# Five units of two down-projections computed with seven block products instead of eight

## The chip, the cores and the metric

The kernel runs on one core of a Trainium2 chip. The metric is the device time of one execution in microseconds, as the median of three runs. Engines are named as the profile names them: PE (TensorE, matrix products), DVE (VectorE), ACT (ScalarE), POOL (GpSimd) and SP (which only issues transfers here). A weight load on TensorE has a row of its own, PEld.

## What is computed

The reference is a small decoder trunk in float32 on 256 tokens of 1024 features: a layer with block-sparse attention, then a layer with sliding-window attention that reads shared keys and values, and behind each attention a channel mixer. The change touches only the last product of the channel mixer:

```python
def conv_ffn(h, w_up, conv_w, conv_b, w_down):
    S_ = h.shape[1]
    u = h @ w_up                                   # 1024 -> 2 x 2816
    up = jnp.pad(u, ((0, 0), (CONV_W - 1, 0), (0, 0)))
    u = conv_b + sum(conv_w[j] * up[:, j:j + S_] for j in range(CONV_W))
    gate, val = jnp.split(u, 2, axis=-1)
    return (jax.nn.silu(gate) * val) @ w_down      # 2816 -> 1024

for l in range(DEPTH):
    ...
    x = x + o.transpose(0, 2, 1, 3).reshape(B_, S_, N_HEADS * HEAD_DIM) @ w_o
    x = x + conv_ffn(rmsnorm(x, ffn_norm[l]), w_up[l], conv_w[l], conv_b[l], w_down[l])
return rmsnorm(x, final_norm)
```

## The kernel before

**Numbers in two parts.** TensorE multiplies in a 32-bit format of reduced precision (fp32r). Every operand is therefore split: a high part, the value rounded to fp32r, and a low part, the rest. A product takes three matmuls: high x high, high x low, low x high. ScalarE makes high parts (`hi_part`, L181, for weights), VectorE low parts (`lo_part`, L189; L191 where a gain is multiplied in).

**Weights in units.** All weights are packed on the host into units of 128 x 2048 floats. SP fetches a unit into one of three raw buffers (`fetch`, L166 to L170). `prepare` (L197) queues its splitting in two or four cuts. The high and low parts lie in four buffers each (`weights`, L193), so a unit's parts can be made once the unit four before it is used up: `used(i)` (L219) calls `prepare(i + 4)`, and `need(i)` sees to it that a unit's steps are queued before TensorE reads it. `w_time` (L203) spaces the due times of units by 4500 ns of the model's clock or more.

**Order.** The program is written by one pass that keeps a model's clock: `tick` advances it by the length of the matmuls issued, `chain` queues steps of the other engines with a delay each, and a step is written down when the clock passes its due time; `require` forces a chain that is needed now. From attention on, the framework's scheduler may take ready instructions of an engine earlier than they were written. Each engine runs its own list in order.

**A mixer** (`ffn`, L661). 22 up units: each gives 128 gate and 128 value features for all 256 tokens, in 48 matmuls of 256 columns (L680 to L682) into a bank of PSUM (tags `u`, `t`, at first `acc`). `post` (L700) takes the convolution and the gate: ScalarE L715, VectorE L719 and L721, ScalarE's silu L725, the product on GpSimd L726, then its high part on ScalarE (L730) and its low part on VectorE (L731), into a quad: a buffer of 128 x 1024 floats in the pool `qd`, which has 15 of them. A quad `pq` holds the parts of two up units. The scaled input of the mixer lies in four more quads until the last up unit has read it.

**A down-projection** (`Down`, L569). 11 units; unit i holds two blocks of 128 rows (k = 0, 1) of `w_down`, 1024 columns each, in two halves (n = 0, 1). The 256 tokens are two blocks (b = 0, 1). So a unit is eight products of 128 x 128 by 128 x 512: A(b,k) B(k,n), summed over k and over all units into four banks `acc[b][n]`. `mm` (L576) writes three matmuls of 512 columns for each (L587, L588, L590); `units` runs through units 0 to 8 and `finish` (L601) takes units 9 and 10 in an order that completes one bank after the other. `add` (L652, instruction L656) adds a bank to the residual `xr[b]`, and `after` starts the next norm: squares (L321), transposes (L288), the split (L297, L298). Behind the first mixer follows the projection of keys and values (L345 to L347) with two weight units of its own; behind the second the final norm: POOL multiplies by the gain (L1057), rstd (L330), ScalarE writes one half of the output (L1068), and `tail` (L1071) the last quarter.

**Names.** `U_DN0` and `U_DN1` number the first units of the two down-projections, `U_KV` the units behind the first. `bank(tag)` hands out PSUM banks: two `u`, two `t`, four `acc`. `mid()` hands out 128 x 512 buffers.

Of the kernel before, what the change touches and what calls it, by code (L numbers as in the profile page):

```python
# [14 lines left out]
P = 128  # L15
# [37 lines left out]
U_KV = U_DN0 + NF // 2  # L53
# [4 lines left out]
N_UNITS = U_DN1 + NF // 2  # L58
# [3 lines left out]
def trunk(ctx: ExitStack, tc, x, xw, pos, cpk, fin, w, out):  # L62
# [116 lines left out]
    def hi_part(i, c):  # L179
        g = gain_of(i, c)  # L180
        nc.scalar.activation(wq[i][0][:, c], raws[i][:, c], AF.Copy, **({} if g is None else {"scale": g}))  # L181

    def lo_part(i, c):
        g, raw, hi, lo = gain_of(i, c), raws[i][:, c], f(wq[i][0][:, c]), wq[i][1][:, c]
# [12 lines left out]
    def prepare(i):  # L197
# [371 lines left out]
    class Down:  # L569


        def __init__(self, u, n_u, parts, wait, short=False):
            self.u, self.n_u, self.parts, self.wait, self.short = u, n_u, parts, wait, short
            self.acc = None

        def mm(self, i, k, b, cols, last=1):  # L576
            if self.acc is None:
                self.acc = [[bank("acc") for _ in range(2)] for _ in range(NB)]
            need(self.u + i)
            self.wait(i)  # L580
            hi, lo = wq[self.u + i]
# [10 lines left out]

        def units(self, lo, hi):
            for i in range(lo, hi):
                for k in range(2):
# [3 lines left out]
                used(self.u + i)  # L599

        def finish(self, i0, after, tail=None, by_half=False):  # L601
# [26 lines left out]
            for i in range(i0, self.n_u):  # L628
                used(self.u + i)

        def end(self, b, n, tail):
# [5 lines left out]
            need(self.u + i)  # L637
            self.wait(i)
            wh, wl = wq[self.u + i]
# [21 lines left out]
    def ffn(layer, u_up, u_dn, hT, y, rb, after, tail=None):  # L661
# [38 lines left out]
        def post(i, up, pq):  # L700
            hi, lo = pq[:, 2 * (i % 2)], pq[:, 2 * (i % 2) + 1]
            t = [row3(S) for _ in range(2)]
            gs, h = row3(S), row3(S)
# [24 lines left out]
            steps = [(200.0, scale), (700.0, tap2)] if i < n_raw else [(200.0, tap2)]  # L728
            chain(("p", i), *steps, (400.0, taps), (1600.0, gate),
                  (3400.0, lambda: nc.scalar.activation(hi, h, AF.Copy)),  # L730
                  (450.0, lambda: nc.vector.tensor_tensor(out=lo, in0=h, in1=f(hi), op=ALU.subtract)))  # L731
            parts.append((hi, lo))

# [10 lines left out]
        for i in range(2, NF):  # L744
            if i % 2 == 0:
                pq = quad()
# [5 lines left out]
        def wait(i):  # L752
            require("p", 2 * i)
            require("p", 2 * i + 1)

        if tail is not None:
            nc.sync.dma_start(fin_t, fin.partition_broadcast(P))
        dn = Down(u_dn, NF // 2, parts, wait, tail is not None)
# [347 lines left out]
def pack(inp):  # L1106
# [20 lines left out]
    def rows2(mat):  # L1127
        mm = k_major(mat)
        for i in range(mm.shape[0] // 2):
            units.append(turns(mm[2 * i:2 * i + 2]).transpose(1, 0, 2).reshape(P, UNIT))  # L1130
# [61 lines left out]
```

## Time and profile before

| | us |
|---|---|
| three runs, median (lowest to highest) | 547.5 (547.49 to 548.63) |
| profiled execution, span from first to last instruction | 545.6 |
| PE busy in that span | 537.5 |
| VectorE / ScalarE / GpSimd busy | 416.9 / 372.6 / 131.6 |
| granted TensorE clock, mean | 0.998 |

The profiled execution is one of its own; what is known of its time is its span, 1.9 us under the median of the runs. Rows of the profile give line, engine, operation, the written and read buffers by the program's names, the shape, and count; then busy time in total, the mean of one in ns, and the idle time before with what ended it. Rows of the order of time begin with the start and the length in us, and end with the idle time before, in brackets. A matmul's length is its latency: matmuls overlap, so what one costs is the distance between starts.

### The profile page before, as it was taken

The page shows a single profiled execution, that of the slowest core. Times are in us where ns is not written, and L with a number is a line of the kernel's source. Part 1 is how long each engine was busy: PE and PEld are TensorE (multiplying, and loading weights), DVE is VectorE, ACT ScalarE, POOL GpSimd, SP SyncE. Part 2 cuts the span into 40 slices and gives each one's busy share as a digit, 9 for nine tenths or more (in the row PEclk, how much of TensorE's full clock was granted, in tenths as well). Part 3 has the DMA queues.
Part 4 walks back from the last instruction along what each step waited for, and adds up shares of the span by engine and source line. Part 5 has one row for each costly group of instructions (what it writes and reads, how often), then busy time and mean ns, then how long its engine had stood idle before and what let it go on. Part 6 is the DMA issues. An engine that isn't in the chain of part 4 may idle for free.

```text
span 545.6 us, 9917 instructions
## 1 busy us (share of the span) xinstructions
PE 537.5 (99%) x3742; PEld 493.9 (91%) x3742; DVE 416.9 (76%) x868; ACT 372.6 (68%) x731; POOL 131.6 (24%) x166
## 2 busy tenths in 40 slices
PE   8999999999999999999999999999999999999995
PEld 7888888899999999988888887789999999998884
DVE  6798778689798888864467788799899888884414
ACT  6989776678577777744357798797567777663314
POOL 8322102013322233220001165202332332210003
PEclk9999999999999999999999999999999999999999
DMA  8974445342556565666553534242375656666201
GB/s 317 401 268 175 167 154 181 129 155 79 199 211 217 223 220 195 208 227 231 178 208 135 179 150 156 77 155 91 142 264 201 214 193 217 249 229 220 109 0 77
DMA packets 16464, 100.99 MB, mean 185 GB/s; under 512 B 1952, under 2 KB 2080, under 8 KB 5920
## 3 DMA queue, kind: packets, MB, share of 16 engines
q1 hardware_dynamic: 16128, 100.09, 50.8%
q8 instruction: 29, 0.48, 0.3%
q10 hardware_dynamic: 288, 0.26, 0.1%
q14 instruction: 19, 0.16, 0.1%
HBM read 99.30 MB, written 1.05 MB: 184 GB/s over the span
## 4 chain that ended last, share of the span: by engine, by line
PE 90%; ACT 5%; DVE 3%; issue 1%; DMA 1%; DVEq 0%; POOL 0%; ACTq 0%
PE acc L590 8%; PE acc L587 8%; PE acc L588 8%; PE u L681 7%; PE u L682 7%; PE u L680 6%; PE t L681 6%; PE t L682 6%; PE t L680 6%; PE acc L345 5%; PE acc L346 5%; PE acc L347 5%; ACT m L468 2%; PE acc L792 2%; PE acc L682 2%; PE acc L681 2%
## 5 line engine op out<-in xcount | busy, mean ns | idle before, releaser
L189 DVE TENSOR_TENSOR wl<-wr,wh 128x1024 fp32r<-128x1024 f32 (+1 forms) x186 | 202.4, 1108 | 49.0 <-ACT wh L181 48.7
L181 ACT ACTIVATE wh<-wr 128x1024 fp32r<-128x1024 f32 (+1 forms) x190 | 176.5, 957 | 50.3 <-PE acc L590 42.2
L726 POOL TENSOR_TENSOR m<-m,m 128x256 f32<-128x256 f32 x44 | 69.1, 1571 | 167.8 <-DVE m L721 89.4
L587 PE MATMUL acc<-wh,q 128*128 128x512 f32 x238 | 92.2, 387 | 0.2 <-ACT q L545 0.2
L588 PE MATMUL acc<-wl,q 128*128 128x512 f32 x238 | 90.6, 381 | 0.0
L680 PE MATMUL u<-q,wh 128*128 128x256 f32 x320 | 88.3, 277 | 0.0
L681 PE MATMUL u<-q,wh 128*128 128x256 f32 x320 | 88.2, 276 | 0.1
L682 PE MATMUL u<-q,wl 128*128 128x256 f32 x320 | 87.9, 275 | 0.0
L680 PE MATMUL t<-q,wh 128*128 128x256 f32 x288 | 79.2, 275 | 0.0
L681 PE MATMUL t<-q,wh 128*128 128x256 f32 x288 | 79.2, 275 | 0.0
L682 PE MATMUL t<-q,wl 128*128 128x256 f32 x288 | 79.2, 275 | 0.0
L590 PE MATMUL acc<-wh,q 128*128 128x512 f32 x238 | 74.9, 380 | 0.0
L681 PEld LDWEIGHTS u<-q,wh 128*128 128x128 f32 x320 | 61.4, 192 | 0.3 <-DVE q L309 0.3
L682 PEld LDWEIGHTS u<-q,wl 128*128 128x128 f32 x320 | 61.4, 192 | 0.0
L680 PEld LDWEIGHTS u<-q,wh 128*128 128x128 f32 x320 | 61.3, 192 | 0.0
L680 PEld LDWEIGHTS t<-q,wh 128*128 128x128 f32 x288 | 55.3, 192 | 0.0
L681 PEld LDWEIGHTS t<-q,wh 128*128 128x128 f32 x288 | 55.3, 192 | 0.0
L682 PEld LDWEIGHTS t<-q,wl 128*128 128x128 f32 x288 | 55.3, 192 | 0.0
L587 PEld LDWEIGHTS acc<-wh,q 128*128 128x128 f32 x238 | 45.0, 189 | 7.0 <-ACT q L545 0.6
L590 PEld LDWEIGHTS acc<-wh,q 128*128 128x128 f32 x238 | 44.8, 190 | 6.2 <-issue 0.2
L588 PEld LDWEIGHTS acc<-wl,q 128*128 128x128 f32 x238 | 45.1, 189 | 5.8 <-issue 0.2
L345 PE MATMUL acc<-wh,q 128*128 128x512 f32 x128 | 50.0, 391 | 0.0
(182 smaller groups left out, 1008.7 us busy)
## 6 DMA issues: line engine op xcount, KB each, us to landing
wr<-in_w SPq DMA_DIRECT2D x82, 1024.0 KB, 4.8
wr<-in_w SPq DMA_DIRECT2D x16, 512.0 KB, 6.2
first<-in_xw SPq DMA_DIRECT2D x7, 384.0 KB, 6.0
xr<-in_x SPq DMA_DIRECT2D x2, 512.0 KB, 7.9
fin_t<-in_fin SPq DMA_DIRECT2D x1, 512.0 KB, 5.7
out<-ot SPq DMA_DIRECT2D x1, 512.0 KB, 2.6
first<-in_xw SPq DMA_DIRECT2D x1, 388.0 KB, 3.5
out<-m ACTq DMA_DIRECT2D x1, 256.0 KB, 2.1
```

Source lines behind the costliest of these rows:

```text
L181: nc.scalar.activation(wq[i][0][:, c], raws[i][:, c], AF.Copy, **({} if g is None else {"scale": g}))
L189: nc.vector.tensor_tensor(out=lo, in0=raw, in1=hi, op=ALU.subtract)
L345: nc.tensor.matmul(o, xh[:, blk(b)], wh, start=(c == 0), stop=False)
L346: nc.tensor.matmul(o, xh[:, blk(b)], wl, start=False, stop=False)
L347: nc.tensor.matmul(o, xl[:, blk(b)], wh, start=False, stop=(c == KC - 1))
L587: nc.tensor.matmul(o, ph[:, blk(b)], turns(hi[:, s_]), start=first, stop=False)
L588: nc.tensor.matmul(o, ph[:, blk(b)], turns(lo[:, s_]), start=False, stop=False)
L590: nc.tensor.matmul(o, pl[:, blk(b)], turns(hi[:, s_]), start=False, stop=end)
L680: nc.tensor.matmul(o, hi[:, s_], xh, start=(c == 0), stop=False)
L681: nc.tensor.matmul(o, hi[:, s_], xl, start=False, stop=False)
L682: nc.tensor.matmul(o, lo[:, s_], xh, start=False, stop=(c == KC - 1))
L726: nc.gpsimd.tensor_tensor(out=h, in0=gs, in1=t[1], op=ALU.mult)
```

## The change

Two units of the first down-projection (3 and 6) and three of the second (3, 6 and 8) form the 2 x 2 by 2 x 2 block product with seven block products in place of eight, in Winograd's form. The seven operands on the left are four blocks of activations and four differences of them (one more block is used as it is); on the right the unit's blocks and four sums of them. Four of the seven products go into four banks of their own (`u`, `t`, `u`, `t`), which collect over all such units of a layer; three go straight into `acc`. After the last such unit `gather` combines the four banks and adds them to the residual: one ScalarE, five VectorE and three GpSimd instructions of 512 columns.

The sums of weights are a unit of their own in the numbering, with high and low parts in a pair of the same buffers, but are not fetched: VectorE makes them from the raw unit before it into two quads of the pool of activations (`sums_of`: one instruction of 2 x 512 columns, two of 512). `slot` maps a unit to its number, `RAW` the numbers to the fetched units. The unit behind one of sums falls due 2500 ns after it instead of 4500.

For these units `post` leaves the product unsplit in a float32 quad, `mix` makes four 128 x 128 differences on GpSimd, and `split` makes high and low part of all eight blocks at once (128 x 1024 on ScalarE and on VectorE) at a set time in the down-projection.

```diff
-U_KV = U_DN0 + NF // 2
+SEVEN = ((3, 6), (3, 6, 8))
+U_KV = U_DN0 + NF // 2 + len(SEVEN[0])
...
+SUMS = [slot(l_, i_) + 1 for l_ in range(2) for i_ in SEVEN[l_]]
...
     def fetch(i):
-        if i < N_UNITS:
+        if i < N_UNITS and i not in SUMS:
...
-                nc.sync.dma_start(raws[i][:, c], w[i][:, c])
+                nc.sync.dma_start(raws[i][:, c], w[RAW[i]][:, c])
+    def sums_of(i):
+        src = raws[i - 1].rearrange("p (k n) -> p k n", k=4)
+        def both():
+            raws[i] = [quad(F32, "sums").rearrange("p c t -> p (c t)") for _ in range(2)]
+            tc.keep_in_program_order(nc.vector.tensor_tensor(out=raws[i][0].rearrange("p (k n) -> p k n", k=2), in0=src[:, 0:3:2],
+                                                             in1=src[:, 3:4].to_broadcast([P, 2, 512]), op=ALU.add))
+        def more(to, a, k):
+            nc.vector.tensor_tensor(out=raw_of(i, half(to)), in0=raw_of(i, half(a)), in1=src[:, k], op=ALU.add)
+        chain(("t", i), (500.0, both), (900.0, lambda: more(2, 0, 2)), (600.0, lambda: more(3, 2, 1)))
...
-        w_time[0] = max(clock[0] + 200.0, w_time[0] + 4500.0, 34000.0 if i == 7 else 0.0)
+        w_time[0] = max(clock[0] + 200.0, w_time[0] + (2500.0 if i - 1 in SUMS else 4500.0), 34000.0 if i == 7 else 0.0)
         def first():
+            if i in SUMS:
+                require("t", i)
...
         def last():
             lo_part(i, cut[-1])
-            fetch(i + 3)
+            if i + 1 in SUMS:
+                require("t", i + 1)
+            if i not in SUMS:
+                fetch(NEXT[i])
+            if i + 2 in SUMS:
+                sums_of(i + 2)
...
+        def seventh(self, i):
+            u = self.at(i)
+            need(u)
+            need(u + 1)
+            self.wait(i)
+            if not self.more:
+                self.more = [bank(t) for t in ("u", "t", "u", "t")]
+            one, five, six, sev = self.more
+            (rh, rl), (th, tl) = wq[u], wq[u + 1]
+            xh, xl = self.parts[2 * i]
+            (a00, a01), (a10, _) = self.acc
+            own = dict(start=i == SEVEN[self.layer][0], stop=i == SEVEN[self.layer][-1])
+            for o, x_, hi, lo, k, mine in ((one, 0, rh, rl, 0, True), (six, 6, th, tl, 2, True), (five, 5, th, tl, 0, True),
+                                           (sev, 4, th, tl, 1, True), (a00, 2, rh, rl, 1, False), (a01, 7, rh, rl, 2, False),
+                                           (a10, 3, th, tl, 3, False)):
+                o, wh, wl = pairs(o), turns(hi[:, half(k)]), turns(lo[:, half(k)])
+                c = blk(x_)
+                nc.tensor.matmul(o, xh[:, c], wh, start=mine and own["start"], stop=False)
+                nc.tensor.matmul(o, xh[:, c], wl, start=False, stop=False)
+                nc.tensor.matmul(o, xl[:, c], wh, start=False, stop=mine and own["stop"])
+                tick(3 * 512 / 2.4)
+            if own["stop"]:
+                self.gather()
+        def gather(self):
...
+            chain(("more",), (100.0, lambda: nc.scalar.activation(v_, one, AF.Copy)),
+                  (100.0, add(dve, x00, one, x00)), (500.0, add(dve, v_, six, v_, ALU.subtract)),
+                  (500.0, add(dve, w_, five, v_)), (400.0, add(pool, x01, x01, w_)),
+                  (100.0, add(dve, z_, sev, v_, ALU.subtract)), (100.0, add(dve, x11, x11, sev, ALU.subtract)),
+                  (400.0, add(pool, x10, x10, z_)), (400.0, add(pool, x11, x11, w_)))
...
             steps = [(200.0, scale), (700.0, tap2)] if i < n_raw else [(200.0, tap2)]
+            if seven:
+                chain(("p", i), *steps, (400.0, taps), (1600.0, gate), *([(1500.0, lambda: mix(pq))] if i % 2 else []))
+                parts.append(pq)
+                return
...
+        def mix(pq):
+            x = pq.rearrange("p c (b t) -> p (c b) t", b=NB)
+            for o, a, b in ((4, 0, 1), (5, 1, 3), (6, 0, 5), (7, 2, 6)):
+                nc.gpsimd.tensor_tensor(out=x[:, o], in0=x[:, a], in1=x[:, b], op=ALU.subtract)
+        def split(i):
+            raw, hi, lo = parts[2 * i], quad(), quad()
+            def high():
+                wait(i, False)
+                nc.scalar.activation(hi, raw, AF.Copy)
+            parts[2 * i] = tuple(t.rearrange("p c t -> p (c t)") for t in (hi, lo))
+            chain(("a", i), (5000.0 * (i - 2) + 300.0, high),
+                  (800.0, lambda: nc.vector.tensor_tensor(out=lo, in0=raw, in1=f(hi), op=ALU.subtract)))
```

The packing on the host changes the order of the four blocks in these five units, and the count of fetched units stays as it was.

More of the change, by code (lines that the diff above doesn't have):

```diff
@@ L57, with slot @@
 U_DN1 = U_UP1 + NF
-N_UNITS = U_DN1 + NF // 2
+N_UNITS = U_DN1 + NF // 2 + len(SEVEN[1])
+def slot(layer, i):
+    return (U_DN0, U_DN1)[layer] + i + sum(k < i for k in SEVEN[layer])
+SUMS = [slot(l_, i_) + 1 for l_ in range(2) for i_ in SEVEN[l_]]
+RAW = {}
+for k_ in range(N_UNITS):
+    if k_ not in SUMS:
+        RAW[k_] = len(RAW)
+NEXT = {k_: min((j_ for j_ in RAW if RAW[j_] == n_ + 3), default=N_UNITS) for k_, n_ in RAW.items()}
 @with_exitstack
@@ L569, in trunk, with __init__ @@
     class Down:
-        def __init__(self, u, n_u, parts, wait, short=False):
-            self.u, self.n_u, self.parts, self.wait, self.short = u, n_u, parts, wait, short
-            self.acc = None
+        def __init__(self, u, n_u, parts, wait, short=False, layer=None):
+            self.u, self.n_u, self.parts, self.wait, self.short, self.layer = u, n_u, parts, wait, short, layer
+            self.acc, self.more = None, None
         def mm(self, i, k, b, cols, last=1):
@@ new lines, in gather, with add @@
+        def gather(self):
+            one, five, six, sev = self.more
+            v_, w_, z_ = (mid() for _ in range(3))
+            (x00, x01), (x10, x11) = ([xr[b][:, half(n)] for n in range(2)] for b in range(NB))
+            def add(eng, out, a, b, op=ALU.add):
+                return lambda: eng.tensor_tensor(out=out, in0=a, in1=b, op=op)
+            dve, pool = nc.vector, nc.gpsimd
+            chain(("more",), (100.0, lambda: nc.scalar.activation(v_, one, AF.Copy)),
[3 more added lines that the diff above has]
+                  (400.0, add(pool, x10, x10, z_)), (400.0, add(pool, x11, x11, w_)))
@@ L593, in units @@
         def units(self, lo, hi):
             for i in range(lo, hi):
+                if self.layer is not None and i in SEVEN[self.layer]:
+                    self.seventh(i)
+                    used(self.at(i))
+                    used(self.at(i) + 1)
+                    yield 21 * 512 / 2.4
+                    continue
                 for k in range(2):
@@ L745, in ffn @@
             if i % 2 == 0:
-                pq = quad()
+                pq = quad(F32 if i // 2 in SEVEN[layer] else F32R)
             up = bank("acc" if i < 4 else "t" if i % 2 else "u")
@@ L750, in ffn, with wait @@
             post(i, [up[:, :S], up[:, S:]], pq)
-        def wait(i):
+        def wait(i, whole=True):
             require("p", 2 * i)
             require("p", 2 * i + 1)
+            if whole and i in SEVEN[layer]:
+                require("a", i)
         if tail is not None:
             nc.sync.dma_start(fin_t, fin.partition_broadcast(P))
-        dn = Down(u_dn, NF // 2, parts, wait, tail is not None)
+        dn = Down(u_dn, NF // 2, parts, wait, tail is not None, layer)
+        for i in SEVEN[layer]:
+            split(i)
         for _ in dn.units(0, NF // 2 - 2):
```

40 lines of the change are left out of this document (26 added, 14 removed).

## The prediction

> **What bounds the kernel now.** I read the page first: busy times, the slices, the chain that ended last.
>
> ```profile
> PE 537.5 (99%) x3742; PEld 493.9 (91%) x3742; DVE 416.9 (76%) x868; ACT 372.6 (68%) x731; POOL 131.6 (24%) x166
> PEclk9999999999999999999999999999999999999999
> PE 90%; ACT 5%; DVE 3%; issue 1%; DMA 1%; DVEq 0%; POOL 0%; ACTq 0%
> ```
>
> TensorE is on 90% of the chain at full clock. But the share is a mean over stages, so the second view is the busy time of each engine in the two stretches that the change touches: the first nine units of each down-projection.
>
> ```profile
> 230.30:277.40 47.10, 47.10 (x222) 41.28 (x221) 24.74 (x28) 20.66 (x26) 4.72 (x10) 1.00 0.58 203
> 482.00:529.10 47.10, 47.10 (x222) 41.30 (x221) 22.10 (x24) 18.07 (x21) 1.47 (x2) 1.00 0.38 135
> ```
>
> The columns after the length are PE, PEld, DVE, ACT, POOL. TensorE has no gap; VectorE, ScalarE and GpSimd are idle for about half of it or more. The third view is the order of time on TensorE and on ScalarE there.
>
> ```profile
> 277.60 0.38 PE L590 MATMUL acc<-wh,q 128*128 128x512 f32 x1
> 282.78 0.38 PE L590 MATMUL acc<-wh,q 128*128 128x512 f32 x1
> ...
> 241.11 2.00 ACT L181 ACTIVATE wh<-wr 128x1024 fp32r<-128x1024 f32 x2 [2.72 <-PE acc L590]
> 246.29 2.00 ACT L181 ACTIVATE wh<-wr 128x1024 fp32r<-128x1024 f32 x2 [3.18 <-PE acc L590]
> 251.47 2.00 ACT L181 ACTIVATE wh<-wr 128x1024 fp32r<-128x1024 f32 x2 [3.18 <-PE acc L590]
> ```
>
> The 0.38 us of a matmul is its latency; its price is the spacing. From 277.60 to 282.78 lie 24 matmuls of 512 columns, three to a product, eight products: 5.18 / 24 = 0.216 us each. They write one bank three times in a row, as the new products do. ScalarE, which makes the high half of a weight unit, starts every 5.18 us and waits each time for TensorE to give a buffer back: weights are prepared four units ahead and wait for TensorE, not the other way. So a matmul taken out of these stretches shortens the kernel by its full spacing, as long as the preparation keeps its lead.
>
> **What goes.** Five units (3 and 6 of the first down-projection, 3, 6 and 8 of the second) take 21 matmuls instead of 24. 5 x 3 = 15 fewer, 15 x 0.216 = 3.24 us: 1.30 in the first layer, 1.94 in the second. The Trainium skill (TensorE: Matmul & The Clock Gate, section Back-to-back issue gap) states about 131 ns per matmul of 512 columns for a stream of weight load and matmul pairs, and 216 as the isolated gap; by the first the saving would be about 1.97 us, an estimate from that page. This trace shows 0.216 in a stream of pairs, so the row decides.
>
> **What comes: weights.** A seven-product unit needs a second unit of sums: 2048 columns more to sum, round and subtract.
>
> ```profile
> L189 DVE TENSOR_TENSOR wl<-wr,wh 128x1024 fp32r<-128x1024 f32 x142 | 173.7, 1238 | 43.1 <-ACT wh L181 43.0
> L181 ACT ACTIVATE wh<-wr 128x1024 fp32r<-128x1024 f32 x146 | 151.0, 1053 | 46.1 <-PE acc L590 40.5 <-PE t L681 2.5 <-PE u L681 1.2
> L189 DVE TENSOR_TENSOR wl<-wr,wh 128x512 fp32r<-128x512 f32 x44 | 28.7, 686 | 5.8 <-ACT wh L181 5.6
> L731 DVE TENSOR_TENSOR q<-m,q 128x256 fp32r<-128x256 f32 x44 | 18.4, 421 | 19.9 <-ACT q L730 19.9
> L730 ACT ACTIVATE q<-m 128x256 fp32r<-128x256 f32 x44 | 18.1, 415 | 43.6 <-POOL m L726 43.5
> ```
>
> VectorE, per such unit: sums 1.24 + 2 x 0.69 = 2.6 (one instruction of 1024 columns, two of 512), low halves 2 x 1.24 = 2.5, the low half of the eight activation blocks 1.2, less two of L731 that go (0.8): 5.5 us. ScalarE: 2 x 1.05 + 1.05 - 0.8 = 2.3 us. The first instruction of the sums reads one block twice and the others with a stride; no row shows that, so it lies between 0.69 and about twice 1.24; I take 1.24, the row of its width.
>
> What hides this is the lead. I lay the second layer out from the start of its down-projection (0), with 5.18 us a unit and 4.53 for seven products. Unit 3 starts at 15.5, unit 6 at 30.4, unit 8 at 40.1. A unit of sums takes one of the four weight buffers, so both buffers of a unit are free at: unit 3 at 5.2, unit 6 at 20.1, unit 8 at 35.0. VectorE's queue at the start is seen in the first layer:
>
> ```profile
> 231.72 1.33 DVE L189 TENSOR_TENSOR wl<-wr,wh 128x1024 fp32r<-128x1024 f32 x1 [0.65 <-ACT wh L181]
> 238.50 1.22 DVE L189 TENSOR_TENSOR wl<-wr,wh 128x1024 fp32r<-128x1024 f32 x1
> 242.20 2.36 DVE L189 TENSOR_TENSOR wl<-wr,wh 128x1024 fp32r<-128x1024 f32 x2 [2.48 <-ACT wh L181]
> ```
>
> The down-projection starts at 230.55 (row below), so VectorE is nearly full until 239.7, then waits. With the sums (2.6) and the split of the activations (1.2) on top it has all for unit 3 at about 13, 2.5 us ahead. For unit 6: buffers at 20.1, high half 1.0, two units' low halves 4.9, split 1.2: 27.7, 2.7 ahead. For unit 8: after unit 7's weights (30.1) come sums to 32.7, first unit to 35.1, split to 36.4, second unit to 38.8: 1.3 ahead. These are the leads that hide the work; when one is gone, TensorE waits by what is missing. I take 0. Upper bound: if VectorE runs slower beside GpSimd, as here,
>
> ```profile
> 226.37 1.67 DVE L189 TENSOR_TENSOR wl<-wr,wh 128x1024 fp32r<-128x1024 f32 x1 [0.31 <-ACT wh L181]
> 221.15 1.68 POOL L726 TENSOR_TENSOR m<-m,m 128x256 f32<-128x256 f32 x1 [3.39 <-DVE m L721]
> 226.22 0.73 POOL L726 TENSOR_TENSOR m<-m,m 128x256 f32<-128x256 f32 x1 [3.39 <-DVE m L721]
> L463 POOL TENSOR_TENSOR m<-m 128x128 f32<-128x128 f32 x16 | 8.0, 505 | 12.9 <-ACT m L468 12.8
> ```
>
> (1.67 against 1.22: 0.45 for one GpSimd instruction beside it), six such hits between unit 6 and unit 8 cost 2.7, less the 1.3: 1.4 us late.
>
> **Activation blocks.** GpSimd makes four 128x128 differences per unit behind the product of the odd up unit. Nearest rows: 0.5 us (L463) to 1.68 us each (twice the width, VectorE busy): 2 to 6.7 us, against 3.39 idle before each product now. In the worst case the next product comes 3.3 us late and ScalarE, which waits in order for it before it rounds the next weights, slips as far. The lead there, on GpSimd, VectorE and TensorE at the end of the first up stage:
>
> ```profile
> 211.27 1.55 POOL L726 TENSOR_TENSOR m<-m,m 128x256 f32<-128x256 f32 x1 [3.39 <-DVE m L721]
> 216.21 1.55 POOL L726 TENSOR_TENSOR m<-m,m 128x256 f32<-128x256 f32 x1 [3.39 <-ACT m L715]
> 214.43 1.21 DVE L189 TENSOR_TENSOR wl<-wr,wh 128x1024 fp32r<-128x1024 f32 x1
> 225.19 0.28 PE L680 MATMUL t<-q,wh 128*128 128x256 f32 x1
> 230.55 0.38 PE L587 MATMUL acc<-wh,q 128*128 128x512 f32 x1
> ```
>
> The helpers' rhythm is 4.94 us a unit, TensorE's 5.36 (from the first matmul of the last up unit to the first of the down-projection), so the lead grows by 0.4 a unit. The last up unit's weights are done at 214.43 + 1.21, 9.5 us before their use, so at unit 8, thirteen units earlier, the lead is about 4. I take 0. The Trainium skill (SBUF — State Buffer, section SBUF: two separate sides) speaks against the change here: GpSimd and a VectorE instruction with two SBUF inputs hold a port pair exclusively, the second fully blocked. The rows 0.73 and 1.68 agree that they hold each other up.
>
> **The gathering.** At the end of units 6 and 8 come one ScalarE copy, five VectorE and three GpSimd instructions of 512 columns.
>
> ```profile
> L321 ACT ACTIVATE m<-xr 128x512 f32<-128x512 f32 x19 | 12.3, 646 | 17.5 <-DVE xr L656 17.3
> L636 DVE TENSOR_TENSOR xr<-acc,xr 128x512 f32<-128x512 f32 x1 | 0.7, 692 | 0.5 <-PE acc L590 0.5
> L1057 POOL TENSOR_TENSOR xf<-xr,fin_t 128x512 f32<-128x512 f32 x3 | 3.8, 1288 | 45.3 <-PE acc L590 45.1 <-issue 0.2
> 528.97 0.38 PE L587 MATMUL acc<-wh,q 128*128 128x512 f32 x1
> 533.95 2.52 POOL L1057 TENSOR_TENSOR xf<-xr,fin_t 128x512 f32<-128x512 f32 x2 [45.15 <-PE acc L590]
> 537.16 0.55 POOL L330 TENSOR_TENSOR rstd<-st,mhalf 128x1 f32<-128x1 f32 x1 [0.69 <-DVE st L329]
> 537.74 1.34 ACT L1068 ACTIVATE ot<-xf,rstd 128x512 f32<-128x512 f32 x2 [1.04 <-POOL rstd L330]
> ```
>
> 0.65 + 5 x 0.69 + 3 x 1.29. In the first layer two whole units hide it. In the second it meets the tail, where ScalarE waits for GpSimd's rstd and so does the end. Unit 8 ends at 528.97, where unit 9's first matmul starts. If nothing of the gathering starts sooner, GpSimd gets its first operand 0.69 x 3 = 2.1 us later and is done at 5.9 after unit 8; its next work, L1057, comes at 5.0, so 0.9 late; two of those end at 8.5 and rstd, due at 8.2, is 0.3 late. The first product is complete 18 matmuls (3.9 us) before the unit ends, so the copy and two VectorE instructions can lie ahead: 0. I take 0, bounds 0 and 0.3. The banks it holds (two u, two t) are needed 5 us later or more.
>
> **Order of preparation.** By the planner's constants a unit of sums falls due 4.5 us after the one before it and the next 2.5 after that: 7.0 where TensorE takes 4.53. Two of them put the due times of the K/V units back by about 5 us.
>
> ```profile
> 277.37 2.56 ACT L181 ACTIVATE wh<-wr,cp 128x512 fp32r<-128x512 f32 x4 [2.62 <-PE acc L590]
> 278.13 2.74 DVE L191 SCALAR_TENSOR_TENSOR wl<-wr,cp,wh 128x512 fp32r<-128x512 f32 x4 [2.44 <-ACT wh L181]
> 281.25 0.76 DVE L656 TENSOR_TENSOR xr<-acc,xr 128x256 f32<-128x256 f32 x2 [0.39 <-PE acc L590]
> ```
>
> Now this runs in the hole before the residual add. Set into the norm's chain it could hold the adds up by its 2.74; if the scheduler fills the hole as before, 0. I take 0, since both engines have nothing else ready at 277.4. SP's queue gets no new transfer; sums are not fetched, and a raw buffer is held one sum longer, with 3.2 us of slack per unit (ScalarE's waits).
>
> **Sum.** The span of 545.6 lies 1.9 us under the median 547.5 of the runs. 545.6 - 3.24 + 0 = 542.4 of span, 544.3 us as a run. Unknown costs: 0 to 1.4 (unit 8), 0 to 0.3 (tail), 0 to 2.7 (K/V); no reason for a gain beyond the matmuls, except that order on the other engines changes: 0.6 either way, an estimate from the tail's own waits (1.04 and 0.69 above).
>
> **The rivals.**
> 1. *VectorE becomes the bound late in the second layer, or the K/V preparation meets the norm.* For: 22.1 + 3 x 5.5 = 38.6 us of VectorE in 45.2, and a lead of 1.3. Against: 15% still free. Costs 1.0 to 2.7: 545.3 to 547.0.
> 2. *The pool of activations is full (slower).* It has 15 quads; at the end of the up stage four hold the scaled input and eleven the products. The sums take two more there. If they have to wait until the last up matmul gives its input back, VectorE stands in order in front of them, up to one up unit (5.35 us), and behind it are taps, low halves, and the split. VectorE has, until unit 3, 15.5 us less 8.6 + 2.4 for work of now less 3.8 new: 0.8 spare, 3.2 if unit 4's weights may come later. From there each microsecond of waiting costs one, per layer: 5.35 - 3.2 = 2.1 to 5.35 - 0.8 = 4.5, twice: 4.3 to 9.1, so 548.6 to 553.4. Against: the eleventh pair's quad is written last, so one is free when the sums begin.
> 3. *A matmul is worth less than its spacing.* If TensorE could overlap these matmuls further, and what they add were only the load of their weights,
>
> ```profile
> L587 PEld LDWEIGHTS acc<-wh,q 128*128 128x128 f32 x238 | 45.0, 189 | 7.0 <-ACT q L545 0.6 <-issue 0.5
> ```
>
> 15 x 0.189 = 2.8 would come off: 544.7. Against: 0.216 over 24 in a row. By the figure of the Trainium skill's page above, 0.131, it would be 545.5, an estimate.
> 4. *The seven products do not come shorter*: each new product waits for a split or a bank and the unit keeps its 5.18: 547.5. For: a unit now needs two weight units and a split. Against: the leads above.
>
> **How the numbers follow.** A measurement of this kernel can tell about 0.2% (1.1 us) from no change. Forecast 0.72 (its own range 543.7 to 545.0), rival 1 0.13, rival 2 0.09, rival 3 0.01, rival 4 0.05. Faster: 0.72 + 0.01 + 0.08 of rival 1 = 0.81. Same: 0.05 + 0.05 of rival 1 + 0.01 = 0.11. Slower: 0.08. The range 543.5 to 546.8 takes in the forecast and rival 1 nearly whole; rivals 2 and 4 and a sliver are left out, 0.18.
>
> **What would show it.** Right: 3727 matmuls instead of 3742; TensorE without gaps in both down stages; the second down-projection's start to the last matmul shorter by 1.9, the first by 1.3; VectorE up by about 28 us for the five units and 7 for gathering. Wrong: idle TensorE before the first matmul of a seven-product unit (rival 1 or 4, by the operand that comes last), a VectorE wait ahead of the sums ended by an up matmul (rival 2), a longer stretch between the last down unit and the K/V projection, or rstd later after unit 8 than 8.2 us.

## The result and the profile after

The changed kernel takes 544.56 us (median of four runs, 544.35 to 544.65) beside 547.51 for the kernel before: a ratio of 0.9943, 95% interval 0.993 to 0.9956. The forecast was 544.3. The profiled execution has a span of 542.6 us after 545.6; the forecast was 542.4.

The page of the changed kernel, its busy times, its granted clock and the chain that ended last:

```profile
PE 534.4 (98%) x3727; PEld 491.3 (91%) x3727; DVE 449.2 (83%) x898; ACT 381.6 (70%) x738; POOL 157.2 (29%) x192
...
PEclk9999999999999999999999999999999999999999
...
PE 89%; ACT 5%; DVE 3%; issue 1%; POOL 1%; DMA 1%; DVEq 0%; ACTq 0%; POOLq 0%
```

There are 3727 matmuls, 15 fewer, and 3.1 us less of them. VectorE has 32.3 us more, GpSimd 25.6, ScalarE 9.0, and little of it shows in the chain: TensorE carries 89% of it after 90%, and GpSimd has 1% after 0%. That 1% lies in the tail and is read further down.

The two stretches of before, with their ends moved up by 1.4 and 3.0 us and the start of the second by 2.0 (the columns after the length are PE, PEld, DVE, ACT, POOL):

```profile
230.30:276.00 45.70, 45.70 (x216) 40.07 (x215) 38.81 (x43) 25.97 (x32) 12.65 (x13) 1.00 0.55 187
480.00:526.10 46.10, 46.10 (x222) 40.55 (x221) 40.40 (x46) 26.77 (x33) 4.32 (x2) 1.00 0.42 158
```

TensorE is full in both. VectorE has gone from about half full to 85 and 88%.

Where the time went is read from four marks: the first matmul of the first down-projection, the first of the K/V projection, the first of the second down-projection, and the start of VectorE's last instruction. Before (the first mark, 230.55, stands in the prediction):

```profile
289.02 0.38 PE L345 MATMUL acc<-wh,q 128*128 128x512 f32 x1
482.35 0.38 PE L587 MATMUL acc<-wh,q 128*128 128x512 f32 x1
541.64 0.74 DVE L1092 SCALAR_TENSOR_TENSOR m<-xr,r_t,fin_t 128x512 f32<-128x512 f32 x1
```

After:

```profile
230.60 0.38 PE L631 MATMUL acc<-wh,q 128*128 128x512 f32 x1
287.97 0.38 PE L389 MATMUL acc<-wh,q 128*128 128x512 f32 x1
481.31 0.38 PE L631 MATMUL acc<-wh,q 128*128 128x512 f32 x1
538.65 0.75 DVE L1214 SCALAR_TENSOR_TENSOR m<-xr,r_t,fin_t 128x512 f32<-128x512 f32 x1
```

| stretch, us | before | after | difference | matmuls gone x 0.216 |
|---|---|---|---|---|
| first down-projection to K/V projection | 58.47 | 57.37 | -1.10 | 1.30 |
| K/V projection to second down-projection | 193.33 | 193.34 | 0.01 | 0 |
| second down-projection to VectorE's last instruction | 59.29 | 57.34 | -1.95 | 1.94 |

The second layer gives all that was forecast. The first keeps 0.19 to 0.20 us back. That loss is the one thing to explain; it is too small for whole runs and shows only in stage lengths. The start-up before the up stage moves every mark by up to 0.9 us from one profiled execution to the next, which is why the stretches, and not the spans, are compared below.

### The profile page after: what moved, and what is told of

It reads as the page before. It is cut to its first block, busy times and chain, and to the rows that moved or that the text cites. A ratio compares the mean times of both kernels' runs of the same rounds, so it can differ in the third digit from the quotient of the medians.

```text
span 542.6 us, 9976 instructions
## 1 busy us (share of the span) xinstructions
PE 534.4 (98%) x3727; PEld 491.3 (91%) x3727; DVE 449.2 (83%) x898; ACT 381.6 (70%) x738; POOL 157.2 (29%) x192
## 3 DMA queue, kind: packets, MB, share of 16 engines
HBM read 99.30 MB, written 1.05 MB: 185 GB/s over the span
## 4 chain that ended last, share of the span: by engine, by line
PE 89%; ACT 5%; DVE 3%; issue 1%; POOL 1%; DMA 1%; DVEq 0%; ACTq 0%; POOLq 0%
PE u L775 7%; PE u L776 7%; PE u L774 7%; PE acc L634 7%; PE acc L631 7%; PE acc L632 6%; PE t L775 6%; PE t L776 6%; PE t L774 6%; PE acc L389 5%; PE acc L391 5%; PE acc L390 5%; ACT m L512 2%; PE acc L914 2%; PE acc L775 2%; PE acc L776 2%
## 5 line engine op out<-in xcount | busy, mean ns | idle before, releaser
L216 ACT ACTIVATE wh<-wr 128x1024 fp32r<-128x1024 f32 (+1 forms) x190 | 174.4, 946 | 29.0 <-issue 8.3
L822 POOL TENSOR_TENSOR m<-m,m 128x256 f32<-128x256 f32 x34 | 56.6, 1665 | 127.6 <-DVE m L817 78.1
L631 PE MATMUL acc<-wh,q 128*128 128x512 f32 x198 | 77.1, 389 | 0.2 <-ACT q L589 0.2
L632 PE MATMUL acc<-wl,q 128*128 128x512 f32 x198 | 75.5, 381 | 0.0
L634 PE MATMUL acc<-wh,q 128*128 128x512 f32 x198 | 63.0, 381 | 0.0
L389 PE MATMUL acc<-wh,q 128*128 128x512 f32 x128 | 50.0, 391 | 0.0
L390 PE MATMUL acc<-wl,q 128*128 128x512 f32 x128 | 48.8, 381 | 0.0
L391 PE MATMUL acc<-wh,q 128*128 128x512 f32 x128 | 48.6, 380 | 0.0
L830 ACT ACTIVATE q<-m 128x256 fp32r<-128x256 f32 x34 | 13.9, 416 | 46.2 <-POOL m L822 46.0
```

Of the source, the lines that this page charges most:

```text
L216: nc.scalar.activation(wq[i][0][:, c], raw_of(i, c), AF.Copy, **({} if g is None else {"scale": g}))
L389: nc.tensor.matmul(o, xh[:, blk(b)], wh, start=(c == 0), stop=False)
L390: nc.tensor.matmul(o, xh[:, blk(b)], wl, start=False, stop=False)
L391: nc.tensor.matmul(o, xl[:, blk(b)], wh, start=False, stop=(c == KC - 1))
L631: nc.tensor.matmul(o, ph[:, blk(b)], turns(hi[:, s_]), start=first, stop=False)
L632: nc.tensor.matmul(o, ph[:, blk(b)], turns(lo[:, s_]), start=False, stop=False)
```

## The loss of 0.19 us: what the traces say

TensorE's order in the first layer's finish, before and then after (transposes for the next norm; each row is a start and a length):

```profile
284.85 0.44 PE L288 MATMUL t<-ident,xr 128*128 128x128 f32 x2
```

```profile
283.83 0.41 PE L332 MATMUL t<-ident,xr 128*128 128x128 f32 x2 [0.17 <-DVE q L342]
```

The same two transposes now wait 0.17 us for the split of the first transposed blocks. Two candidates. *VectorE is late*: the low halves of the K/V weights, which filled the hole ahead of the residual adds, now run until 280.3, and the first add starts straight behind them. *A second writer*: three of the four halves of the residual, all but the first, are now last written by GpSimd (gathering), so the add that follows has two engines to wait for. VectorE there, in the changed kernel:

```profile
273.97 6.40 DVE L226 SCALAR_TENSOR_TENSOR wl<-wr,cp,wh 128x512 fp32r<-128x512 f32 x8
280.29 0.74 DVE L750 TENSOR_TENSOR xr<-acc,xr 128x256 f32<-128x256 f32 x2
```

The lines of the residual add and of the square, in 276 to 288 us of the changed kernel, hold instructions that neither line had before:

```profile
L750 DVEq EVENT_SEMAPHORE  x2: 21/21/21, 281.3 to 285.1; - x2
```

```profile
L365 ACTq EVENT_SEMAPHORE  x2: 17/17/17, 282.2 to 286.2; - x2
```

They are waits of their own on the queues of VectorE and ScalarE, in the middle of the norm's chain. The third half has one on each line as well, behind the stretch.

## The experiments

**Is it 0.216 us per matmul, unit by unit?** First, the eighth product is put back with everything else kept:

```diff
-            (a00, a01), (a10, _) = self.acc
+            (a00, a01), (a10, a11) = self.acc
...
-                                           (a10, 3, th, tl, 3, False)):
+                                           (a10, 3, th, tl, 3, False), (a11, 1, rh, rl, 0, False)):
...
-                    yield 21 * 512 / 2.4
+                    yield 24 * 512 / 2.4
```

> The changed kernel with an eighth product of three matmuls put back into each of the five units (it multiplies one activation block with one weight block that do not belong together and adds this to the fourth bank, so the output is another): all the added work stays, the saving goes. Theory (each matmul taken out pays its spacing of 0.216 us, the added work is hidden but for about 0.2 us): 15 x 0.216 = 3.24 us more than the changed kernel, span 545.8, a run 547.8, a hair over the kernel before. Rival (part of the gain comes from the other engines' new order or lighter activation work): clearly under 547.0. Rival (the added work costs TensorE, and the matmuls are worth more than their spacing): clearly over 548.5.

Measured: 547.86 us (547.58 to 548.24), ratio 1.0007 [0.9998, 1.0015]. The stretches are 58.67 and 59.28 where before has 58.47 and 59.29. So all the work that comes with the change, 33 us of VectorE, 23 of GpSimd and 9 of ScalarE by this run's page, costs 0.20 us in the first layer and nothing in the second, and the rest of the gain is the matmuls.

Then each layer alone:

```diff
-SEVEN = ((3, 6), (3, 6, 8))
+SEVEN = ((3, 6), ())
```

> Seven products in units 3 and 6 of the first down-projection alone. Theory: 6 x 0.216 = 1.30 us off, less 0.2 lost where the residual adds of the first mixer meet the late low halves of the K/V weights: span 544.5, a run 546.4. Rival (the loss belongs to the second layer): span 544.3, with the K/V projection reached 1.3 us earlier than before instead of 1.05.

Measured: 546.36 us, ratio 0.9981 [0.9972, 0.999]; stretches 57.38 and 59.29.

```diff
-SEVEN = ((3, 6), (3, 6, 8))
+SEVEN = ((), (3, 6, 8))
```

> Seven products in units 3, 6 and 8 of the second down-projection alone. Theory: 9 x 0.216 = 1.94 us off and nothing lost: span 543.7, a run 545.6. Rival (the loss is in the tail, where GpSimd's adds stand in the chain that ends last): span 543.9 or more.

Measured: 545.77 us, ratio 0.997 [0.9959, 0.9982]; stretches 58.47 and 57.34. The two layers add up: each stretch is that of before where the layer is left alone and that of the change where it is not.

**Which of the two makes the 0.19?** Unit 5 in place of 6 ends the gathering earlier and frees VectorE ahead of the residual add:

```diff
-SEVEN = ((3, 6), (3, 6, 8))
+SEVEN = ((3, 5), (3, 6, 8))
```

> Units 3 and 5 instead of 3 and 6 in the first layer, the second as changed. The gathering comes one unit earlier (5.2 us), so its adds no longer push VectorE's work into the residual adds. Theory: the 0.19 us lost before the K/V projection comes back: span 542.4, a run 544.4; first residual add at 4.1 us after unit 8 as in the kernel before, not 4.4. Rival (one unit between two of seven products is too little lead for VectorE, since a pair needs about 10 us of it in 9.7): TensorE waits ahead of unit 5, span 542.9 or more. Rival (the loss comes from the due times of the K/V units): span 542.6 as it was.

Measured: 544.63 us, ratio 0.995 [0.9937, 0.9962]; the stretch is 57.37 as in the change. The first residual add in this run, and the transposes:

```profile
280.12 0.76 DVE L750 TENSOR_TENSOR xr<-acc,xr 128x256 f32<-128x256 f32 x2 [0.39 <-PE acc L634]
```

```profile
283.93 0.41 PE L332 MATMUL t<-ident,xr 128*128 128x128 f32 x2 [0.17 <-DVE q L342]
```

The add waits for TensorE again, not for VectorE, and the 0.17 stays. The theory that VectorE is late has fallen. GpSimd's last add ends at 269.2 in this run, 10.9 us ahead of the residual add, so the time that GpSimd takes is not the cause either. Next, the second writer is taken away, with VectorE's load raised:

```diff
-            dve, pool = nc.vector, nc.gpsimd
+            dve, pool = nc.vector, nc.vector
```

> The changed kernel with the three residual adds of the gathering on VectorE instead of GpSimd. After units 3 and 5 left the loss where it was, the theory is: the 0.19 us lost ahead of the K/V projection is the price of one more semaphore wait on VectorE and on ScalarE in front of the residual add and the squares of those halves of the residual that GpSimd has written. Then it goes: first down-projection to K/V projection 57.18 us instead of 57.37, span 542.4, no wait instruction of its own at the residual adds. Rival (the loss is VectorE's or ScalarE's load there): VectorE has 2.1 us more to do per gathering, so it stays 0.19 or grows. The tail is unchanged for both (rstd waits for VectorE's sum of squares).

Measured: 544.44 us (544.09 to 544.85), ratio 0.9941 [0.9929, 0.9953]. The first stretch is 57.18, the other 57.34, and the transposes have no wait:

```profile
284.12 0.44 PE L332 MATMUL t<-ident,xr 128*128 128x128 f32 x2
```

The semaphore instructions are gone from both lines, and the whole 0.19 us is back in the stretch: the second writer made the loss. Counted from the first four transposes (281.76 in the change), the second add starts 0.07 us later in the change than before, the square of that half 0.13 and the next transposes 0.22; in this run all three lie as before. In the second layer, where VectorE has two such waits and ScalarE one, they cost nothing: 57.34 with GpSimd's adds and without. In the times of whole runs this version cannot be told from the change (544.44 beside 544.56, with overlapping ranges).

**How much room has VectorE?** Each sum is written twice, 2.65 us more of VectorE per unit (this kernel's lines are two higher):

```diff
-            tc.keep_in_program_order(nc.vector...
+            for _ in range(2):
+              tc.keep_in_program_order(nc.vector...
...
-            nc.vector.tensor_tensor(out=raw_of(i, half(to)), ...
+            for _ in range(2):
+                nc.vector.tensor_tensor(out=raw_of(i, half(to)), ...
```

> The changed kernel with every instruction of the sums of weights issued twice: 2.65 us more of VectorE for each of the five units, same result. Theory (the work is hidden by leads that the trace shows: 3.3 and 3.7 us in the first layer, 2.2, 3.8 and 1.06 in the second): the first layer hides it, in the second unit 3 comes 0.4 and unit 8 up to 1 us late: span 543.0 to 544.1. Rival (VectorE is idle for 12% of the second stage, so all is hidden): 542.6. Rival (VectorE already bounds the stage): 5 x 2.65 more, 555.

Measured: 549.61 us (548.21 to 550.38), ratio 1.003 [1.0019, 1.0041], more than the theory had and less than its last rival; the stretches are 58.58 and 61.80. The first layer, which was to hide the work, does not. It waits at unit 6, and its 1.21 us over the 57.37 of the change lie there:

```profile
263.05 0.48 PE L661 MATMUL u<-wl,q 128*128 128x512 f32 x1 [0.78 <-DVE wl L226]
```

TensorE at unit 6 of the second layer:

```profile
516.34 0.69 PE L661 MATMUL u<-wl,q 128*128 128x512 f32 x1 [1.61 <-DVE wl L226]
516.82 0.63 PE L662 MATMUL u<-wh,q 128*128 128x512 f32 x1
517.25 0.63 PE L661 MATMUL t<-wl,q 128*128 128x512 f32 x1
```

This is the one wait that the trace names in the second layer; it was forecast for units 3 and 8. And it did not come alone. Two stretches of this run around it, with the granted clock after the five engines:

```profile
510.00:514.30 4.30, 4.24 (x20) 3.41 (x19) 4.30 (x6) 1.86 (x3) 0.00 (x0) 1.00 0.08 15
...
516.30:519.80 3.50, 3.46 (x8) 2.76 (x9) 3.50 (x4) 0.00 (x0) 0.00 (x0) 0.53 0.95 393
```

After the wait the clock is 0.53 for 3.5 us, and eight matmuls come 0.43 us apart: 8 x 0.21 = 1.7 us more, nearly as much as the wait. The stall with the gaps ahead of it and the half clock make 3.9 of the 4.5 us that this stretch has over 57.34. Half clock behind a wait had not been reckoned with. The Trainium skill (TensorE: Matmul & The Clock Gate, section Part 1: The HAM clock gate) puts the fall to half clock behind an idle window of about 3.4 us and the return behind as long a busy one. The return is near that (3.5 us here, 4.4 in a run below). The fall does not need so long a gap here: 1.61 us was enough, with gaps of 0.2 and 0.1 us shortly ahead of it.

Then the sums go to GpSimd, which has little to do there:

```diff
-            tc.keep_in_program_order(nc.vector...
+            tc.keep_in_program_order(nc.gpsimd...
...
-            nc.vector.tensor_tensor(out=raw_of(i, half(to)), ...
+            nc.gpsimd.tensor_tensor(out=raw_of(i, half(to)), ...
```

> The changed kernel with the sums of weights on GpSimd. GpSimd needs 2.6 + 2 x 1.29 = 5.2 us for a unit's sums by its row of 512 columns, up to twice that beside a busy VectorE; VectorE gets 2.65 us back. Theory: units 3 and 6 hide it (their sums can start 8 us and more ahead), unit 8 in the second layer does not: its sums end 5 to 10 us after the raw unit's turn while VectorE's end after 2.6: TensorE waits 0 to 3 us: span 542.6 to 545.6. Rival (GpSimd is idle there for 90%, and VectorE is what is short): span 542.6 or less, with a longer lead at unit 8.

Measured: 544.69 us (544.22 to 545.06), ratio 0.9945 [0.9933, 0.9957]; stretches 57.37 and 57.35. No time is won or lost. GpSimd's groups in this run:

```profile
L203 POOL TENSOR_TENSOR sums<-sums,wr 128x512 f32<-128x512 f32 x10 | 18.2, 1825 | 1.9 <-DVE q L850 1.2
L199 POOL TENSOR_TENSOR sums<-wr 128x1024 f32<-128x1024 f32 x5 | 15.5, 3104 | 13.9 <-DVE wl L224 8.5 <-DMA wr<-in_w 5.4
```

A sum takes 3.10 and 1.83 us there instead of VectorE's 1.22 and 0.72 (below). Three such units fit into the leads. But VectorE is not relieved: its busy time is 455.0 us after 449.2 in the change, though the 13 us of sums have gone from it. A run below shows why.

**Can more units follow?** Seven units instead of five:

```diff
-SEVEN = ((3, 6), (3, 6, 8))
+SEVEN = ((3, 5, 7), (2, 4, 6, 8))
```

> Seven products in units 3, 5, 7 of the first and 2, 4, 6, 8 of the second down-projection: 21 matmuls fewer, 4.54 us. Theory: two units of which one is of seven products need 10.6 us of VectorE in 9.7 us of TensorE, so each further pair eats 0.9 us of lead; the first layer starts with 3.3 and gets through (0.65 us gained there), the second starts later than its VectorE queue allows at unit 2 (about 13 us of work in 10.4) and stalls at unit 2 by 1 to 2.5 us and again at 6 and 8: span 542 to 544. Rival (leads suffice): 541.3. Rival (VectorE becomes the bound of both stages): over 545.

Measured: 546.03 us (545.88 to 546.63), ratio 0.9972 [0.9961, 0.9983], a worse time than with five units. The theory had the first layer get through and the second stall at units 2, 6 and 8; it is the first layer that fails. The stretch is 58.63 there, where 56.53 was to be had, and 57.50 in the second layer, where 56.70 was. TensorE's waits in the first:

```profile
282.60 0.83 PE L332 MATMUL t<-ident,xr 128*128 128x128 f32 x4 [1.19 <-DVE xr L750]
...
285.23 0.41 PE L332 MATMUL t<-ident,xr 128*128 128x128 f32 x2 [0.50 <-DVE q L342]
```

and VectorE ahead of them:

```profile
275.81 6.41 DVE L226 SCALAR_TENSOR_TENSOR wl<-wr,cp,wh 128x512 fp32r<-128x512 f32 x8
282.13 1.41 DVE L750 TENSOR_TENSOR xr<-acc,xr 128x256 f32<-128x256 f32 x4
```

Here VectorE *is* late: the eight K/V low halves end 1.9 us later than in the change, and the residual adds wait behind them. In the second layer the wait is 0.48 us at unit 4.

Two more runs take this apart. Four units in the second layer alone, the gathering on VectorE:

```diff
-SEVEN = ((3, 6), (3, 6, 8))
+SEVEN = ((3, 6), (2, 4, 6, 8))
...
-            dve, pool = nc.vector, nc.gpsimd
+            dve, pool = nc.vector, nc.vector
```

> As the run with all three edits, but with the sums of weights on VectorE. Theory (VectorE's queue stalls unit 4): first layer 57.18, second layer 57.2 to 57.5 with a wait of TensorE for a low half of about 0.5 us at unit 4, a run 544.2 to 544.4. Rival (the stall was an accident of the K/V order in the first layer's other run): no wait, 56.70, a run 543.7.

Measured: 544.57 us (544.35 to 545.43), ratio 0.9947 [0.9934, 0.996]; stretches 57.18 and 57.44. TensorE at unit 4, and the engines from the start of the down-projection to unit 8's end:

```profile
502.13 0.38 PE L658 MATMUL u<-wh,q 128*128 128x512 f32 x1
502.95 0.48 PE L659 MATMUL u<-wl,q 128*128 128x512 f32 x1 [0.44 <-DVE wl L224]
503.27 0.38 PE L660 MATMUL u<-wh,q 128*128 128x512 f32 x1
```

```profile
481.40:526.00 44.60, 44.16 (x206) 38.24 (x205) 43.71 (x51) 28.99 (x35) 3.48 (x2) 1.00 0.41 154
```

VectorE is busy for 43.71 of 44.60 us: that is the limit. The rows also price a wait. Between 502.13 and 502.95 lie 0.82 us instead of 0.216, and the next matmul comes after 0.32, so the wait that is counted as 0.44 costs 0.60 + 0.10 = 0.70, about all that the fourth unit's three matmuls bring (0.65). The stretch says the same: 56.70 + 0.70 = 57.40, where 57.44 is measured, beside 57.34 with three units.

And three units in the first layer, with a gathering no later than in the change:

```diff
-SEVEN = ((3, 6), (3, 6, 8))
+SEVEN = ((2, 4, 6), (3, 6, 8))
...
-            dve, pool = nc.vector, nc.gpsimd
+            dve, pool = nc.vector, nc.vector
```

> Units 2, 4 and 6 of the first layer instead of 3 and 6; gathering's adds all on VectorE; sums on VectorE as in the change. Theory A (with units 3, 5, 7 the 1.7 us ahead of the K/V projection came from where the gathering lay: after unit 7, in front of the K/V low halves and the residual adds; VectorE's total of the stage still fits): gathering ends as early as in the change, so start of the first down-projection to the K/V projection is 57.18 - 0.65 = 56.53 us, or 57.0 if unit 4 waits by the 0.45 seen with units 2 and 4 in the second layer; a run 543.7 to 544.1. Theory B (a third unit fills VectorE whichever units they are, so the K/V low halves come late again): 57.5 to 58.6 in that stretch with TensorE waiting for xr, a run 544.7 to 545.8.

Measured: 544.94 us (544.71 to 545.91), ratio 0.9954 [0.994, 0.9968]; the first stretch is 57.62, the second 57.34. The first residual add, then TensorE's only wait in that layer's down-projection and finish:

```profile
280.59 0.76 DVE L750 TENSOR_TENSOR xr<-acc,xr 128x256 f32<-128x256 f32 x2 [0.39 <-PE acc L634]
```

```profile
252.66 0.48 PE L659 MATMUL u<-wl,q 128*128 128x512 f32 x1 [0.82 <-DVE wl L224]
```

The adds wait for TensorE again, so a third unit need not make them late. Theory A put this down to where the gathering lies. That is not shown alone: this run also has the gathering's adds on VectorE, where the run with units 3, 5, 7 had them on GpSimd, and two low halves beside them took 1.93 and 1.71 us there instead of 1.22. Unit 4 waits 0.82, which costs 0.27 more, as the wait of 0.44 cost 0.26 more above: 1.09, and 56.53 + 1.09 = 57.62 is the stretch. The third unit loses 0.44 against the two with the same gathering (57.18).

Last, VectorE is relieved of the sums as well. These were meant as the versions that beat the change:

```diff
-SEVEN = ((3, 6), (3, 6, 8))
+SEVEN = ((3, 6), (2, 4, 6, 8))
...
-            dve, pool = nc.vector, nc.gpsimd
+            dve, pool = nc.vector, nc.vector
...
-            tc.keep_in_program_order(nc.vector...
+            tc.keep_in_program_order(nc.gpsimd...
...
-            nc.vector.tensor_tensor(out=raw_of(i, half(to)), ...
+            nc.gpsimd.tensor_tensor(out=raw_of(i, half(to)), ...
```

> Gathering's three GpSimd adds on VectorE, all sums of weights on GpSimd, and four seven-product units in the second layer (2, 4, 6, 8) instead of three. Theory (the 0.19 us of the first layer is the wait for a second writer; the 0.48 us stall at unit 4 with four units was VectorE's queue, which the sums no longer fill): start of the first down-projection to the K/V projection 57.18 instead of 57.37, start of the second down-projection to the last VectorE instruction 56.70 instead of 57.34, a run 544.56 - 0.19 - 0.64 = 543.7. Rival (the stall at unit 4 was ScalarE's turn, or GpSimd's sums come too late for the denser units): 57.2 to 57.7 in the second layer, a run 544.2 to 544.8.

Measured: 556.58 us (555.72 to 557.09), ratio 1.0162 [1.0149, 1.0175], far above both expectations. The rival had named late sums, at 0.5 to 1.0 us. The first stretch is 57.17 as forecast; the second is 68.63. TensorE at unit 4 and at unit 6, then VectorE and GpSimd ahead of the first:

```profile
509.92 0.80 PE L659 MATMUL u<-wl,q 128*128 128x512 f32 x1 [7.21 <-DVE wl L224]
...
523.87 0.48 PE L659 MATMUL u<-wl,q 128*128 128x512 f32 x1 [1.75 <-DVE wl L224]
```

```profile
502.08 3.36 DVE L224 TENSOR_TENSOR wl<-sums,wh 128x1024 fp32r<-128x1024 f32 x1
505.37 2.29 DVE L224 TENSOR_TENSOR wl<-wr,wh 128x1024 fp32r<-128x1024 f32 x1
507.58 2.29 DVE L224 TENSOR_TENSOR wl<-sums,wh 128x1024 fp32r<-128x1024 f32 x1
```

```profile
497.27 3.81 POOL L203 TENSOR_TENSOR sums<-sums,wr 128x512 f32<-128x512 f32 x2 [3.83 <-DVE q L850]
...
504.44 4.34 POOL L203 TENSOR_TENSOR sums<-sums,wr 128x512 f32<-128x512 f32 x2
```

Two things add up. Unit 4's sums end at 501.08, where VectorE had them at 497.74 in the run with the sums on VectorE: 3.3 us later. And from 502.08 to 509.87 VectorE makes three low halves in 7.8 us that take 3.5 there, because GpSimd's next sums run beside them: 4.3 us more. Between the sums' end and the first of these lie 1.0 us instead of 1.7, so the last low half is 7.0 us later (509.87 beside 502.89), and the wait is 6.8 longer (7.21 beside 0.44). Moving the sums off VectorE did not relieve it: each low half with a GpSimd sum beside it takes nearly twice as long or more (2.29 and 3.36 us for 1.22). The Trainium skill (SBUF — State Buffer, section SBUF: two separate sides) describes an exclusive lock on a port pair shared by the two, and the rows agree, longer on both sides (GpSimd's 2.17 a sum, beside 1.29 for its multiplication of 512 columns in the kernel before). Behind the 7.21 us the clock fell to half for 4.4 us; behind the 1.75 us it did not. Of the 11.93 us that the stretch has over 56.70, the first wait takes 7.6, the half clock 2.3 and the second wait 2.0. Why GpSimd's second sum stood 3.83 us, with VectorE's split named as its releaser, is not settled; without that wait the sums would have ended at 497.25, ahead of VectorE's, so their lateness is not shown to come from GpSimd's slower instructions.

The same with units 3, 5, 7 in the first layer:

> Units 3, 5, 7 of the first and 2, 4, 6, 8 of the second layer, sums on GpSimd, gathering on VectorE. Theory A (the 1.7 us lost ahead of the K/V projection with unit 7 came from GpSimd's slow gathering and the second writer): first layer 57.18 - 0.65 = 56.53, second 56.70, a run 543.1. Theory B (unit 7's gathering and the late low halves of the K/V weights stand in VectorE's queue ahead of the residual adds, whoever sums): first layer 57.5 to 58.6, a run 544.1 to 545.1, with TensorE waiting for xr.

Measured: 558.27 us (557.3 to 562.31), ratio 1.0209 [1.0184, 1.0234]; stretches 59.78 and 67.05. The waits are again for low halves: 0.79, 0.18 and 0.67 us in the first layer, 6.90 and 1.34 in the second. One more, of 0.52 us, is for VectorE's split of the transposed blocks ahead of the K/V projection, and none is for the residual. Theory B's wait for xr did not come, and the first layer is slower than either theory had it: with TensorE held up by the low halves, this run cannot decide between them.

## Why the prediction was right

**The 15 matmuls at 0.216 us.** Right, in each layer alone, with the product put back, and to 0.01 us in the second layer. The last matmuls of unit 8 and the first of unit 9, after:

```profile
525.55 0.38 PE L659 MATMUL acc<-wl,q 128*128 128x512 f32 x1
525.77 0.38 PE L660 MATMUL acc<-wh,q 128*128 128x512 f32 x1
525.99 0.38 PE L631 MATMUL acc<-wh,q 128*128 128x512 f32 x1
```

The spacing in the new units is that of before. Rival 3 (0.189, 2.8 us) and the 131 ns of the Trainium skill (TensorE: Matmul & The Clock Gate, section Back-to-back issue gap), which would have brought 1.97 us, are refuted by the 3.05 us of the stretches.

**VectorE hidden by its lead.** Right for this change, in part by better sizes than assumed. The groups of the new work, after:

```profile
L838 POOL TENSOR_TENSOR q<-q 128x128 f32<-128x128 f32 x20 | 14.4, 719 | 1.6
L672 POOL TENSOR_TENSOR xr<-xr,m 128x512 f32<-128x512 f32 x6 | 10.3, 1747 | 63.8 <-DVE m L672 63.8
L203 DVE TENSOR_TENSOR sums<-sums,wr 128x512 f32<-128x512 f32 x10 | 7.2, 718 | 0.2
...
L199 DVE TENSOR_TENSOR sums<-wr 128x1024 f32<-128x1024 f32 x5 | 6.1, 1215 | 0.0
```

The first sum, bounded by 0.69 and 2.5 us, costs 1.22, close to the 1.24 taken. One count was wrong: VectorE was to have 5.5 us more per unit, and 28 us in all. The seven products take three raw blocks and four sums on the right, and three blocks and four differences on the left. The fourth raw block goes into the sums alone, so it is not split: an instruction of 1024 columns becomes one of 512, which is 1.24 - 0.69 = 0.55 us less for VectorE and 1.05 - 0.64 = 0.41 less for ScalarE. 28 + 7 - 5 x 0.55 = 32.3 is what the page shows, where 35 was said. The last lead of the second layer, the low half that VectorE makes for unit 8 and TensorE's start on it:

```profile
519.24 1.22 DVE L224 TENSOR_TENSOR wl<-sums,wh 128x1024 fp32r<-128x1024 f32 x1
```

```profile
521.46 0.38 PE L658 MATMUL u<-wh,q 128*128 128x512 f32 x1
```

1.0 us, where 1.3 was forecast. The forecast has a slip of 0.5 in it: the terms for unit 6 (20.1 + 1.0 + 4.9 + 1.2) add up to 27.2 and not 27.7, so its terms give 1.8 for unit 8. The half in the row is first read by the unit's fifth matmul, 0.86 us behind the one shown, so TensorE had 1.9 us in hand; the waits for `wl` at bank `u` above stand at that product. The lead is real: 2.65 us more of VectorE per unit (the doubled sums) turn the leads at unit 6 of both layers into stalls.

**GpSimd's differences at nothing.** Right; 0.72 us each, inside the bounds of 0.5 and 1.68, and no wait came of them.

**The gathering at nothing.** Right in the tail, wrong in the first layer. GpSimd in the tail:

```profile
527.03 3.74 POOL L672 TENSOR_TENSOR xr<-xr,m 128x512 f32<-128x512 f32 x3 [36.54 <-DVE m L672]
530.96 2.65 POOL L1179 TENSOR_TENSOR xf<-xr,fin_t 128x512 f32<-128x512 f32 x2 [0.19 <-issue]
534.17 0.55 POOL L374 TENSOR_TENSOR rstd<-st,mhalf 128x1 f32<-128x1 f32 x1 [0.56 <-DVE st L373]
```

Unit 8 ends at 525.99: L1179 comes 4.97 after it (before: 4.98) and rstd 8.2 (before: 8.2). It is tight, with 0.19 us between gathering and L1179, and it held. The chain that ended last now runs through the third of these adds,

```profile
529.54 1.23 POOL xr L672
```

then L1179 and rstd. With all adds on VectorE the stretch is the same 57.34, so this cost nothing. The step that failed is the sentence on the first layer: "two whole units hide it". They hide its engine time and not who wrote the residual last. That cost 0.19 us, and the run with all adds on VectorE gave it back whole.

**The K/V low halves at 0.** Right as a price, which is luck, since the reason was not: they do meet the first residual add (280.3, behind them), and unit 5 in place of 6 shows that this add's delay did not reach TensorE. With unit 7 it did.

**The rivals.** 1 did not happen in the change, but happens with one more unit in either layer. 2 did not: the sums in VectorE's queue had no wait for an up matmul. 4 is refuted by the stretches.

The sum: 545.6 - 3.24 + 0.19 for the second writer + 0.05 of start-up = 542.6, the span of the profiled execution.

## What to carry to other kernels

When one engine carries 90% of the chain, fewer instructions on it are worth their spacing, unit by unit, for as long as each helper's total in that stage and its lead at each unit both hold; add up both, since here VectorE at 87 to 88% held and at 98% gave a wait that ate the next unit's gain. Before giving a relieving job to another engine, look at what the two do to each other: GpSimd's sums made VectorE's instructions beside them nearly twice as long. And when a short step is handed to an idle engine, ask who reads the result on the critical chain: a second writer is a second wait there. Here it cost 0.19 us in one layer and nothing in the other.

## What the runs showed of the hardware

- A wait of TensorE counted as x cost about x + 0.27 us here (0.44 cost 0.70, 0.82 cost 1.09, 1.75 cost 2.0). The wait is counted from the end of the matmul before, 0.38 - 0.216 = 0.16 us behind the start that was due, and the matmul behind the wait is followed after 0.32 us instead of 0.216.
- TensorE's clock was 0.53 for 3.5 us behind a wait of 1.61 us and about 0.5 for 4.4 us behind one of 7.21 us, and stayed full behind one of 1.75 us. What decides between the short ones stays open.
- VectorE's subtraction of 1024 columns, 1.22 us, takes 2.29 or more beside GpSimd's sums. GpSimd's add of 512 columns in gathering was taken at 1.29 and measures 1.75 on average, and its sum of 1024 columns takes 3.10.
- A wait for a second engine shows as a semaphore instruction of 17 to 21 ns. Four of them lay in the norm's chain where TensorE lost 0.19 us, and went with the loss. That the second writer is the cause is shown, and that the delay begins at the add behind the first of them (0.07 us); whether these instructions themselves carry it, or the signal they wait for, is open.
